# Expert weights in slots of 16 KB a partition, with the contraction order permuted to match

## The chip, the cores and the metric

The kernel runs on one core of one Trainium2 chip. The metric is the device time of one execution in microseconds (us). Profile times are counted from the first instruction. TensorE is called PE, VectorE DVE, ScalarE ACT, GpSimd POOL, and SyncE, which issues the large loads, SP. MiB are 1,048,576 bytes; the profile's MB are millions of bytes.

## The reference, cut to what matters

One residual block on 256 tokens of width 1024, all in float32: a mixer (gated linear attention beside banded attention, projections of 1024 x 8208 and 1024 x 1024), then 32 experts, then a small gated embedding and a norm.

```python
xn = rmsnorm(x, ln_mix); z = xn @ w_in            # mixer: w_in is 1024 x 8208
x = x + (sigmoid(gA) * y_a + sigmoid(gB) * y_b) @ w_out
xm = rmsnorm(x, ln_moe)                           # top 4 of 32 experts per token
for e in range(32):                               # w1[e]: 1024 x 2048, w2[e]: 1024 x 1024
    h = xm @ w1[e] + b1[e]
    out += gates[:, e:e+1] * (clamped_swiglu(h) @ w2[e] + b2[e])
x = x + out
x = x + sigmoid(rmsnorm(x, ln_ple) @ w_ple_gate) * (p @ w_ple_proj)
out = rmsnorm(x, ln_final)
```

An expert has 8 MiB of `w1` and 4 MiB of `w2`; the 32 have 384 MiB, all read once.

## The kernel before, in words

Each expert takes the up to 64 tokens that chose it. For expert e the order on PE, written out by hand, is: the bias (`h`, L750); the first layer (`h`, L758), 64 matmuls over eight slabs k of 128 rows of `w1`; transposes of small selectors (`t_st`); the scatter of expert e-1 (`acc`, L812); the gather of tokens for the next pair of experts (`t_g`, L725); the transposes of the activation (`t_a`, L776); and the second layer (`y`, L786), 32 matmuls over `w2`. Between `h` and `t_a` stands the gated unit on DVE and ACT (`glu`, L764 to L770).

Weights come through slots: SBUF tiles of 8 KB a partition (1 MiB), taken in a fixed cycle `order` from six pools (`N0` to `N5`: 1 + 5 + 3 + 4 + 6 + 2 = 21 slots). A slot of `w1` is one slab: partition p holds row 128k + p, one run of 8 KB in DRAM. A slot of `w2` holds two slabs: partition p holds rows p and p + 128 of a block of 256, two runs of 4 KB. SP issues all these loads in the program's order (L705 where a slot has two runs, L707 where it has one), and a load waits until the slot's last reader is done. The SBUF behind most slots belongs to the mixer's tiles first; `load_ahead` fills six slots while the mixer runs (L280), and the others come free as the mixer ends. The projections of the mixer stream through five of the same slots, in halves of a unit of 512 columns (`unit_steps`, L222; `out_weights`, L578). In the mixer's last part `out_prep(1)` transposes the second half of the gated sum (`t_h`, L567) and splits it into `hb`.

Expert 30 is preceded by the projection of `p` (`ple_proj`: `t_pT`, `t_pp`); the gate weights (4 MiB) follow expert 31, and `tail` does the rest. The branch for experts with more than 64 tokens (L1094) is not taken.

Of the kernel before, what the change touches and what calls it, by code (L numbers as in the profile page):

```python
# [64 lines left out]
def block_kernel(ctx: ExitStack, tc: tile.TileContext, x, p, ln_mix, w_in, w_gk, b_gk, gla_norm, rel_rev,  # L65
# [9 lines left out]
    ring0 = ctx.enter_context(tc.tile_pool(name="ring0", bufs=N0))  # L75
# [32 lines left out]
    # loads are issued in the order of the program  # L108
# [5 lines left out]
    # ------------------------------------------------------------------ mixer  # L114
    with ExitStack() as px:
# [12 lines left out]
        # the order of allocation puts what ends early under the slots that the experts take first  # L128
        # a place in the order of allocation for what comes to be allocated later
# [14 lines left out]
        lnr = wk.tile([16, P], F32, name="lnr")  # L144
# [29 lines left out]
        for i, a in enumerate((ln_moe, ln_ple)):  # L174
            nc.scalar.dma_start(lnr[8 * i:8 * i + 8, :], a.rearrange("o (k p) -> (o k) p", p=P))
# [7 lines left out]
        nc.gpsimd.dma_start(wr, w_router[0].rearrange("(k p) e -> p k e", p=P))  # L183
# [112 lines left out]
        with tc.tile_pool(name="gl", bufs=1, side="right") as gl:  # L296
# [15 lines left out]
            # low-rank forget gate  # L312
# [107 lines left out]
            load_ahead(N0, ring0)  # L420
# [118 lines left out]
        for i in range(4):  # L539
# [5 lines left out]
                                                         bhi[64:128, :].bitcast(F32), op=ALU.subtract))  # L545
        t0 = pa("t_ln2")
        nc.tensor.transpose(t0[:, 0:16], lnr, ident[0:16, 0:16])
        nc.vector.tensor_copy(lnT[:, 8:24], t0[:, 0:16])
# [63 lines left out]
        # residual, router  # L612
# [9 lines left out]
        def route_T(tb, half):  # L622
            t = pp("t_1")[:, 0, :].rearrange("p (k t) -> p k t", k=4)
            for j in range(4):
                k = 4 * half + j
                nc.tensor.transpose(t[:, j, :], x_sb[:, tb, k * P:k * P + P], ident)
            (nc.scalar.copy if half else nc.vector.tensor_copy)(x1T[tb][:, 4 * half:4 * half + 4, :], t)
# [58 lines left out]
    # ------------------------------------------------------------------ experts  # L686
# [8 lines left out]
    rest_of = [ring4, ring4, ring, ring4, ring, ring4, ring, ring4, ring4, ring, ring] + [ring3] * N3  # L695
    order = itertools.chain(rest_of, itertools.cycle([ring0] * N0 + [ring2] * N2 + [ring5] * N5 + rest_of))

    def slot_tile(dt, nm, pool=None):
        return (pool or next(order)).tile([P, 2048], dt, name=nm, tag="w")

    def slot(src, pool=None):
        w = slot_tile(F32, "w_raw", pool)
        n = src.shape[0] // P
        if n > 1:
            nc.sync.dma_start(w.rearrange("p (k c) -> p k c", k=n), src.rearrange("(k p) c -> p k c", p=P))  # L705
        else:
            nc.sync.dma_start(w, src)  # L707
        return w

    def expert_weights(e, k0=0):  # L710
        es_ = slice(e, e + 1) if isinstance(e, int) else bass.ds(e, 1)
        return ([slot(w1[0, es_, k * P:k * P + P, :].rearrange("o p c -> (o p) c")) for k in range(k0, KC)]
                + [slot(w2[0, es_, k * 256:k * 256 + 256, :].rearrange("o p c -> (o p) c")) for k in range(4)])
# [448 lines left out]
```

## Time and profile before

| | us |
|---|---|
| median of 3 runs | 1260.97 (1260.8 to 1262.39) |
| span of the profiled execution | 1259.5 |
| PE busy | 1151.8 (91%) |
| DVE busy | 374.1 (30%) |
| ACT busy | 262.8 (21%) |
| POOL busy | 37.2 (3%) |

The span is from the first instruction's start to the last one's end in the profiled execution; that execution's own time is not among the three runs, which stand 1.3 to 2.9 us above its span. A busy share is an average over stages with different limits: the mixer takes up to about 285 us, the experts up to 1220, the tail the rest.

### The profile page before, as it was taken

To read this page: it belongs to the slowest core of one execution; us is meant where nothing else is said; L and a number is where in the kernel's file an instruction comes from. 1 tells how busy PE (TensorE), PEld (TensorE's weight loads), DVE (VectorE), ACT (ScalarE), POOL (GpSimd) and SP (SyncE) were. 2 spreads that over 40 slices of the span, in tenths; PEclk is the share of its full clock that TensorE was granted. 3 is DMA by queue.
4 is the path that set the end of the run, shared out by engine and by line. 5 is a ranking of instruction groups with operands and counts; after the bars stand their busy time and mean duration, and the time that the engine had idled before them with its cause. 6 is when DMAs were issued, how large, how long until landed. Compare 5 with 4: busy or idle time off the path is not lost.

```text
span 1259.5 us, 15242 instructions
## 1 busy us (share of the span) xinstructions
PE 1151.8 (91%) x6314; PEld 575.8 (46%) x6314; DVE 374.1 (30%) x699; ACT 262.8 (21%) x464; POOL 37.2 (3%) x88
## 2 busy tenths in 40 slices
PE   6999999999999999999888888888888888888996
PEld 6988978874333433333333333333333333333345
DVE  5687476553111212112211111111111111111135
ACT  4756465541000100001000000000000000001025
POOL 2001010000000000000000000000000000000000
PEclk8999999989899999999999999999999999999898
DMA  9769778778999999999999999999999999999980
GB/s 279 223 124 287 218 152 224 283 286 340 395 419 416 416 416 417 417 416 417 417 417 417 417 417 418 417 417 417 417 417 417 418 417 417 417 416 417 417 325 35
DMA packets 95033, 454.32 MB, mean 361 GB/s; under 512 B 8488, under 2 KB 8656, under 8 KB 62192
## 3 DMA queue, kind: packets, MB, share of 16 engines
q1 hardware_dynamic: 91744, 447.51, 91.8%
q0 software_dynamic: 1840, 5.39, 1.7%
q8 instruction: 51, 0.84, 0.3%
q10 hardware_dynamic: 1376, 0.41, 0.2%
q14 instruction: 22, 0.18, 0.0%
HBM read 452.23 MB, written 1.05 MB: 360 GB/s over the span
## 4 chain that ended last, share of the span: by engine, by line
PE 58%; DMA 37%; ACT 2%; DVE 2%; issue 1%; SPq 0%; ACTq 0%
DMA w_raw<-in_w_dram 35%; PE h L758 16%; PE y L786 11%; PE t_g L725 4%; PE acc L812 2%; PE u_gB L247 2%; PE ax L592 2%; PE t_gate L1005 2%; PE u_ka L247 2%; DMA w_raw<-in_w_ple_gate_dram 2%; PE u_vg L251 1%; PE u_va L251 1%; PE u_qa L247 1%; PE u_gA L251 1%; PE u_qg L242 1%; ACT aT L778 1%
## 5 line engine op out<-in xcount | busy, mean ns | idle before, releaser
L758 PE MATMUL h<-w_raw,xT 128*64 128x512 f32 x2048 | 467.9, 599 | 54.8 <-DMA w_raw<-in_w_dram 54.8
L758 PEld LDWEIGHTS h<-w_raw,xT 128*64 128x64 f32 x2048 | 134.8, 136 | 370.5 <-issue 218.2
L786 PE MATMUL y<-w_raw,aT 128*64 128x512 f32 x1024 | 231.4, 605 | 23.0 <-ACT aT L778 23.0
L764 DVE TENSOR_SCALAR xg<-h 128x512 f32<-128x512 f32 x32 | 22.1, 692 | 495.6 <-PE h L758 495.6
L786 PEld LDWEIGHTS y<-w_raw,aT 128*64 128x64 f32 x1024 | 71.8, 139 | 162.4 <-issue 130.9
L803 ACT ACTIVATE jg<-t_st 128x256 f32<-128x256 f32 x32 | 12.3, 386 | 531.3 <-PE t_st L800 531.3
L791 DVE SCALAR_TENSOR_TENSOR yl<-y,gs,yh 128x512 fp32r<-128x512 f32 x32 | 24.0, 751 | 263.0 <-ACT yh L789 263.0
L126 DVE TENSOR_TENSOR wl<-w_raw,wh 128x1024 fp32r<-128x1024 f32 x68 | 83.2, 1224 | 49.9 <-ACT wh L126 49.5
L126 ACT CAST wh<-w_raw 128x1024 fp32r<-128x1024 f32 x68 | 71.2, 1047 | 68.0 <-PE u_ka L247 9.0
L789 ACT ACTIVATE yh<-y,gs 128x512 fp32r<-128x512 f32 x32 | 22.0, 688 | 234.6 <-PE y L786 234.6
L725 PE MATMUL t_g<-oh,x_sb 128*128 128x128 f32 x512 | 67.2, 287 | 0.0
L725 PEld LDWEIGHTS t_g<-oh,x_sb 128*128 128x128 f32 x512 | 61.6, 197 | 10.8 <-issue 10.2
L745 POOL CAST zs<-cb 128x128 fp32r<-128x128 f32 x32 | 9.5, 296 | 940.6 <-PE h L750 844.0
L778 ACT COPY aT<-t_a 128x512 f32<-128x512 f32 x32 | 18.8, 586 | 86.0 <-PE t_a L776 86.0
L812 PE MATMUL acc<-yh,st 64*128 64x512 f32 x124 | 28.2, 447 | 0.0
L812 PE MATMUL acc<-yl,st 64*128 64x512 f32 x124 | 25.2, 398 | 0.0
L729 DVE TENSOR_TENSOR xT<-t_g,lnT 128x512 f32<-128x512 f32 x32 | 22.1, 692 | 7.7 <-PE t_g L725 3.9
L750 PE MATMUL h<-BH,zs 128*128 128x512 f32 x64 | 24.2, 461 | 0.0
L797 DVE TENSOR_SCALAR go<-cb,posm,gates 128x128 f32<-128x128 f32 x64 | 21.6, 342 | 2.0 <-PE acc L870 2.0
L770 DVE TENSOR_TENSOR xlin<-xlin,sgm 128x512 f32<-128x512 f32 x32 | 21.9, 685 | 0.2
L769 DVE SCALAR_TENSOR_TENSOR xlin<-xlin,xg 128x512 f32<-128x512 f32 x32 | 21.8, 682 | 0.0
L768 DVE TENSOR_SCALAR xlin<-h 128x512 f32<-128x512 f32 x32 | 21.8, 681 | 0.0
(388 smaller groups left out, 1141.2 us busy)
## 6 DMA issues: line engine op xcount, KB each, us to landing
w_raw<-in_w_dram SPq DMA_DIRECT2D x384, 1024.0 KB, 19.9
w_raw<-in_w_in_dram SPq DMA_DIRECT2D x32, 1024.0 KB, 9.8
w_raw<-in_w_out_dram SPq DMA_DIRECT2D x4, 1024.0 KB, 4.9
w_raw<-in_w_ple_gate_dram SPq DMA_DIRECT2D x4, 1024.0 KB, 20.2
BT<-in_rel_bias_dram POOLq DMA_DIRECT2D x8, 256.0 KB, 6.6
x_sb<-in_x_dram SPq DMA_DIRECT2D x2, 512.0 KB, 5.0
BT<-in_rel_bias_dram POOLq DMA_DIRECT2D x8, 128.0 KB, 4.0
w_raw<-in_w_ple_proj_dram SPq DMA_DIRECT2D x1, 1024.0 KB, 20.8
```

Source lines behind the costliest of these rows:

```text
L126: return nc.scalar.copy(hi, full), nc.vector.tensor_tensor(lo, full, hi.bitcast(F32), op=ALU.subtract)
L247: nc.tensor.matmul(av[:, c, :], wt[:, kk % 2, c * P:c * P + P], xt[:, k, :], start=first and c % 2 == 0, stop=last, skip_group_check=True)
L251: nc.tensor.matmul(av[:, tb, :], xt[:, k, tb * P:tb * P + P], wt[:, kk % 2, :], start=first, stop=last)
L592: nc.tensor.matmul(ax[tb][dh], ht[:, tb, j, :], wt[:, dh * 512:dh * 512 + 512], start=hf == 0 and j == 0 and pi == 0, stop=hf == 1 and j = ...
L725: nc.tensor.matmul(t, x_sb[:, tb, k * P:k * P + P], oh[:, tb, :], start=first and tb == 0, stop=tb == 1, skip_group_check=True)
L750: nc.tensor.matmul(h[:, bk, :], zsel, BH[:, bk * 512:bk * 512 + 512], start=True, stop=False, skip_group_check=True)
L758: nc.tensor.matmul(h[64 * half:64 * half + 64, bk, :], stat(k), ws[k][:, c:c + 512], start=False, stop=k == KC - 1, skip_group_check=True)
L778: nc.scalar.copy(aT, t.rearrange("p (c s) -> p c s", c=4))
L786: nc.tensor.matmul(y[64 * dh:64 * dh + 64, :], aT[:, kk % 4, 64 * (kk // 4):64 * (kk // 4) + 64], w[:, kk % 2, dh * 512:dh * 512 + 512], s ...
L791: nc.vector.scalar_tensor_tensor(yl, y, gs, yh.bitcast(F32), op0=ALU.mult, op1=ALU.subtract)
L812: nc.tensor.matmul(dst[tb][dh], st[64 * dh:64 * dh + 64, tb * P:tb * P + P], y[64 * dh:64 * dh + 64, :], start=first and i == 0, stop=last ...
L1005: nc.tensor.matmul(t, xp[:, k, tb * P:tb * P + P], gp, start=k == 0 and i == 0, stop=k == KC - 1 and i == 2)
```

## The change

Slots become 16 KB a partition (2 MiB): ten of them (3 + 1 + 2 + 3 + 1), and 8 KB aside in `ring2` for `b2s` and `lfb`. One load fills a slot, and partition p takes neighbouring rows: 2p and 2p + 1 of a block of 256 rows of `w1`, 4p to 4p + 3 of a block of 512 rows of `w2`. In DRAM that is one run of 16 KB for each partition. An expert has six loads instead of twelve. The order of the contraction is permuted to match (`cols`): slab k now holds every second row, so the operands on the other side (`x_sb` in the gather and the router's transposes, `ln_moe` and `ln_ple`, the router's weights, `x2` and `y` in the transposed scatter) are read with a step of two, and the gated unit writes `a` with a step of four undone (`glu`). The projections of the mixer and `w_out` still come in 1 MiB loads, two to a slot. The matmuls are as many as before, and PE's order is the same up to the tail.

```diff
-N0, N1, N2, N3, N4, N5 = 1, 5, 3, 4, 6, 2
-AHEAD = (8, 12, 16)
+N1, N2, N3, N4, N5 = 3, 1, 2, 3, 1
+AHEAD = (8,)
+RJ = 2
+KM = KC // RJ
...
+    def cols(k, base=0):
+        m, j = divmod(k, RJ)
+        return slice(base + m * P * RJ + j, base + (m + 1) * P * RJ, RJ)
...
+            raws = ring.tile([P, KC, 512], F32, name="w_raw", tag="w")
             for half in range(2):
-                raw = ring.tile([P, 4, 512], F32, name="w_raw", tag="w")
+                raw = raws[:, 4 * half:4 * half + 4, :]
...
-                w = pool.tile([P, 2048], F32, name="w_raw", tag="w")
-                nc.sync.dma_start(w, w1[0, 0, k * P:k * P + P, :])
+                w = pool.tile([P, 4096], F32, name="w_raw", tag="w")
+                nc.sync.dma_start(w, w1[0, 0, k * 256:k * 256 + 256, :].rearrange("(p j) c -> p (j c)", j=RJ))
...
-            load_ahead(N0, ring0)
...
+        lnr = wk.tile([2 * KM, P * RJ], F32, name="lnr", tag="hf")
+        for i, a in enumerate((ln_moe, ln_ple)):
+            nc.gpsimd.dma_start(lnr[KM * i:KM * i + KM, :], a.rearrange("o (m q) -> (o m) q", m=KM))
...
-    rest_of = [ring4, ring4, ring, ring4, ring, ring4, ring, ring4, ring4, ring, ring] + [ring3] * N3
-    order = itertools.chain(rest_of, itertools.cycle([ring0] * N0 + [ring2] * N2 + [ring5] * N5 + rest_of))
+    rest_of = [ring4, ring, ring4, ring4, ring, ring] + [ring3] * N3
+    order = itertools.chain(rest_of, itertools.cycle([ring2] * N2 + [ring5] * N5 + rest_of))
...
+    def halves(dt, *nms):
+        w = slot_tile(dt, nms[0])
+        return w[:, 0:2048], w[:, 2048:4096]
+
+    def slot(src):
+        w = slot_tile(F32, "w_raw")
+        nc.sync.dma_start(w, src.rearrange("(p j) c -> p (j c)", p=P))
         return w
...
-            nc.tensor.matmul(t, x_sb[:, tb, k * P:k * P + P], oh[:, tb, :], start=first and tb == 0, stop=tb == 1,
+            nc.tensor.matmul(t, x_sb[:, tb, cols(k)], oh[:, tb, :], start=first and tb == 0, stop=tb == 1,
...
-                    c = half * 1024 + bk * 512
-                    nc.tensor.matmul(h[64 * half:64 * half + 64, bk, :], stat(k), ws[k][:, c:c + 512],
+                    c = k % RJ * 2048 + half * 1024 + bk * 512
+                    nc.tensor.matmul(h[64 * half:64 * half + 64, bk, :], stat(k), ws[k // RJ][:, c:c + 512],
...
-        nc.vector.tensor_tensor(xl_, xl_, sg, op=ALU.mult)
-        return xl_
+
+        a = mo.tile([P, 4, P], F32, name="a", tag="xg", bufs=1)
+        nc.vector.tensor_tensor(a, xl_.rearrange("s (p c) -> s c p", c=4), sg.rearrange("s (p c) -> s c p", c=4),
+                                op=ALU.mult)
+        return a
...
-        b2s = slot_tile(F32, "b2s")[0:NE, 0:D]
+        b2s = ring2.tile([P, 2048], F32, name="b2s", tag="s")[0:NE, 0:D]
...
-        return [slot(w_ple_gate[0, k2 * 256:k2 * 256 + 256, :]).rearrange("p (k c) -> p k c", k=2) for k2 in range(4)]
+        raw = []
+        for k4 in range(2):
+            raw.extend(halves(F32, "w_raw"))
+            for k2 in range(2 * k4, 2 * k4 + 2):
+                nc.sync.dma_start(raw[k2], w_ple_gate[0, k2 * 256:k2 * 256 + 256, :].rearrange("(p j) c -> p (j c)", p=P))
+        return [r.rearrange("p (k c) -> p k c", k=2) for r in raw]
```

Two places show how instructions move. The first is SP's queue where the mixer ends and the loads of the experts begin; `w_raw` numbers the slots' tiles, and the names in brackets are the counters a load waits for (`DVE`, `PE`: a reader of what lay in that memory; `DMAHW`: an earlier load). Before, from the last load of `w_out`:

```order
L578 DMA w_raw_2669<-in_w_out_dram 128x2x1024 [waits DMAHW0_49,DVE_49]
L707 DMA w_raw_2842<-in_w1_dram 128x2048 [waits DMAHW1_49,PE_49]
L707 DMA w_raw_2844<-in_w1_dram 128x2048 [waits DMAHW2_49]
L705 DMA w_raw_2846<-in_w2_dram 128x2x1024 [waits DMAHW4_49,DVE_49]
L705 DMA w_raw_2848<-in_w2_dram 128x2x1024 [waits DVE_49]
L705 DMA w_raw_2850<-in_w2_dram 128x2x1024 [waits DMAHW5_49,DVE_49]
L705 DMA w_raw_2852<-in_w2_dram 128x2x1024 [waits DMAHW6_49,PE_49]
L707 DMA w_raw_2991<-in_w1_dram 128x2048 [waits DMAHW7_49,DVE_49]
L707 DMA w_raw_2993<-in_w1_dram 128x2048 [waits DMAHW0_49,DVE_49,PE_49]
L707 DMA w_raw_2995<-in_w1_dram 128x2048 [waits DMAHW1_49,DVE_49]
```

The same place after the change:

```order
L592 DMA w_raw_2633<-in_w_out_dram 128x2x1024
L721 DMA w_raw_2815<-in_w1_dram 128x4096 [waits DVE_49,PE_49]
L721 DMA w_raw_2817<-in_w1_dram 128x4096 [waits DMAHW6_49,DMAHW5_49,DMAHW4_49]
L721 DMA w_raw_2819<-in_w2_dram 128x4096
L721 DMA w_raw_2821<-in_w2_dram 128x4096 [waits PE_49]
L721 DMA w_raw_2961<-in_w1_dram 128x4096 [waits DMAHW7_49,DMAHW0_49]
L721 DMA w_raw_2963<-in_w1_dram 128x4096 [waits DMAHW2_49,DMAHW1_49,DVE_49]
L721 DMA w_raw_2965<-in_w1_dram 128x4096 [waits PE_49]
L721 DMA w_raw_2967<-in_w1_dram 128x4096 [waits PE_49]
L721 DMA w_raw_2969<-in_w2_dram 128x4096 [waits DMAHW3_49,PE_49]
```

Before, the first of these loads waits for a matmul of the linear attention (`t_O`), and the load into `w_raw_2995` is the first to wait for the DVE instruction that finishes `hb`. After, the very first one (`w_raw_2815`) waits for that same DVE instruction, since its larger slot covers that memory too, and all later loads stand behind it.

The second place is ACT at expert 31 and the start of the tail: `yh` is the expert's output as ACT writes it, and `gh` the first split of the gate weights. Before:

```order
L766 ACTIVATE sgm<-xg 128x512
L778 COPY aT<-t_a 128x512
L789 ACTIVATE yh<-y,gs 128x512
L903 ACTIVATE gh<-w_raw,lnT 128x1024
L978 CAST x2h<-x2T 128x512 x2
```

After:

```order
L780 ACTIVATE sgm<-xg 128x512
L795 COPY aT<-t_a 128x512
L924 ACTIVATE gh<-w_raw,lnT 128x1024
L806 ACTIVATE yh<-y,gs 128x512
L999 CAST x2h<-x2T 128x512 x2
```

The split of the gate weights has moved ahead of `yh`, so ACT now reads the first gate weights before it takes the last expert's output.

## Rows read from the trace of the kernel before

**Rows 1.** The page: chain of work that ended last, by engine.
```profile
PE 58%; DMA 37%; ACT 2%; DVE 2%; issue 1%; SPq 0%; ACTq 0%
```

**Rows 2.** Busy time by stretch, last three columns: granted clock, DMA share, GB/s.
```profile
345.00:1145.00 800.00, 725.80 (x3532) 270.41 (x3529) 141.81 (x295) 62.39 (x138) 8.74 (x28) 1.00 1.02 417
```

**Rows 3.** PE's waits, 600 to 1260: us in total, times, longest.
```profile
PE h L758 <- DMA w_raw<-in_w_dram: 53.4, 91, 1.4
```

**Rows 4.** The chain in order of time: start, us, what.
```profile
388.54 7.09 PE y L786 x32
...
414.82 7.09 PE y L786 x32
...
930.13 1.12 PE acc L812 x8
...
960.25 1.13 PE acc L812 x8
```

**Rows 5.** DMA queue of SP, 345 to 1145: packets, MB, share of 16 engines.
```profile
q1 hardware_dynamic: 59404, 332.64, 101.4%
```

**Rows 6.** DMA of two stretches, 604 to 619 and 652.5 to 662.5: all packets, then SP's.
```profile
DMA packets 867, 6.31 MB, mean 421 GB/s; under 512 B 97, under 2 KB 97, under 8 KB 97
...
q1 hardware_dynamic: 867, 6.31, 101.2%
...
DMA packets 1014, 4.09 MB, mean 409 GB/s; under 512 B 63, under 2 KB 63, under 8 KB 968
...
q1 hardware_dynamic: 1013, 4.08, 101.8%
```

**Rows 7.** The page's queues: the one that loads instructions (packets, MB, share).
```profile
q8 instruction: 51, 0.84, 0.3%
```

**Rows 8.** The page's DMA issues: engine, count, KB each, us to landing.
```profile
w_raw<-in_w_dram SPq DMA_DIRECT2D x384, 1024.0 KB, 19.9
w_raw<-in_w_in_dram SPq DMA_DIRECT2D x32, 1024.0 KB, 9.8
w_raw<-in_w_out_dram SPq DMA_DIRECT2D x4, 1024.0 KB, 4.9
...
x_sb<-in_x_dram SPq DMA_DIRECT2D x2, 512.0 KB, 5.0
```

**Rows 9.** DMA queue of SP, 0 to 345.
```profile
q1 hardware_dynamic: 25850, 82.86, 77.1%
```

**Rows 10.** SP's issues by time: start, us, line, operation, count.
```profile
232.26 0.89 SPq L707 DMA_DIRECT2D w_raw<-in_w_dram  x2
...
254.85 0.33 SPq L707 DMA_DIRECT2D w_raw<-in_w_dram  x1
...
272.24 2.65 SPq L707 DMA_DIRECT2D w_raw<-in_w_dram  x3
...
287.00 0.38 SPq L705 DMA_DIRECT2D w_raw<-in_w_dram  x1
```

**Rows 11.** SP's waits, 190 to 300.
```profile
SPq L707 <- DVE hb L126: 1.8, 1, 1.8
```

**Rows 12.** Busy time by stretch, 285 to 288.
```profile
285.00:288.00 3.00, 3.00 (x15) 1.06 (x16) 2.86 (x15) 0.26 (x1) 0.00 (x0) 1.00 0.00 0
```

**Rows 13.** PE's instructions by time, 1113 to 1215; in brackets the idle time before.
```profile
1140.93 1.94 PE L758 MATMUL h<-w_raw,xT 128*64 128x512 f32 x8 [1.19 <-DMA w_raw<-in_w_dram]
...
1182.14 9.88 PE L786 MATMUL y<-w_raw,aT 128*64 128x512 f32 x32 [0.72 <-ACT aT L778]
...
1208.07 3.74 PE L832 MATMUL x2T<-cb,x 128*128 128x128 f32 x32
```

**Rows 14.** Groups by line, 345 to 1145: PE's weight loads, then DVE's.
```profile
L725 PEld LDWEIGHTS t_g<-oh,x_sb 128*128 128x128 f32 x439 | 51.1, 191 | 10.2 <-issue 10.2
...
L770 DVE TENSOR_TENSOR xlin<-xlin,sgm 128x512 f32<-128x512 f32 x27 | 18.5, 685 | 0.0
```

**Rows 15.** POOL's instructions by time, 0 to 345.
```profile
90.51 2.93 POOL L441 DMA_DIRECT2D BT<-in_rel_bias_dram  x4 [58.61 <-PE t_s L402]
```

More of the change, by code (lines that the diff above doesn't have):

```diff
@@ L143, in block_kernel @@
         wr = wk.tile([P, KC, NE], F32, name="wr")
-        lnr = wk.tile([16, P], F32, name="lnr")
+        wk.tile([P, P], F32, name="room0")
         kept("wh", 4)
@@ L545, in block_kernel @@
                                                          bhi[64:128, :].bitcast(F32), op=ALU.subtract))
+        lnr = wk.tile([2 * KM, P * RJ], F32, name="lnr", tag="hf")
+        for i, a in enumerate((ln_moe, ln_ple)):
+            nc.gpsimd.dma_start(lnr[KM * i:KM * i + KM, :], a.rearrange("o (m q) -> (o m) q", m=KM))
         t0 = pa("t_ln2")
-        nc.tensor.transpose(t0[:, 0:16], lnr, ident[0:16, 0:16])
-        nc.vector.tensor_copy(lnT[:, 8:24], t0[:, 0:16])
+        n2 = 2 * KM
+        for j in range(RJ):
+            nc.tensor.transpose(t0[:, j * n2:j * n2 + n2], lnr[:, j::RJ], ident[0:n2, 0:n2])
+        nc.vector.tensor_copy(lnT[:, 8:24].rearrange("p (i j) -> p j i", j=RJ),
+                              t0[:, 0:16].rearrange("p (j i) -> p j i", j=RJ))
         for k in range(KC):
@@ L624, in route_T @@
             for j in range(4):
-                k = 4 * half + j
-                nc.tensor.transpose(t[:, j, :], x_sb[:, tb, k * P:k * P + P], ident)
+                nc.tensor.transpose(t[:, j, :], x_sb[:, tb, cols(4 * half + j)], ident)
             (nc.scalar.copy if half else nc.vector.tensor_copy)(x1T[tb][:, 4 * half:4 * half + 4, :], t)
@@ L693, in pm @@
         return ps.tile([P, 512], F32, name=nm, tag="m", bufs=2)
-    rest_of = [ring4, ring4, ring, ring4, ring, ring4, ring, ring4, ring4, ring, ring] + [ring3] * N3
-    order = itertools.chain(rest_of, itertools.cycle([ring0] * N0 + [ring2] * N2 + [ring5] * N5 + rest_of))
+    rest_of = [ring4, ring, ring4, ring4, ring, ring] + [ring3] * N3
+    order = itertools.chain(rest_of, itertools.cycle([ring2] * N2 + [ring5] * N5 + rest_of))
     def slot_tile(dt, nm, pool=None):
[L699 to L707, printed above, removed]
+        return (pool or next(order)).tile([P, 4096], dt, name=nm, tag="w")
+    def halves(dt, *nms):
[4 more added lines that the diff above has]
+        nc.sync.dma_start(w, src.rearrange("(p j) c -> p (j c)", p=P))
         return w
@@ L711, in expert_weights @@
         es_ = slice(e, e + 1) if isinstance(e, int) else bass.ds(e, 1)
-        return ([slot(w1[0, es_, k * P:k * P + P, :].rearrange("o p c -> (o p) c")) for k in range(k0, KC)]
-                + [slot(w2[0, es_, k * 256:k * 256 + 256, :].rearrange("o p c -> (o p) c")) for k in range(4)])
+        return ([slot(w1[0, es_, k * 256:k * 256 + 256, :].rearrange("o p c -> (o p) c")) for k in range(k0, KM)]
+                + [slot(w2[0, es_, k * 512:k * 512 + 512, :].rearrange("o p c -> (o p) c")) for k in range(2)])
     def one_hots(e):
@@ L783, in second_layer @@
         for kk in range(8):
-            w = ws[8 + kk // 2].rearrange("p (k c) -> p k c", k=2)
+            w = ws[KM + kk // 4].rearrange("p (k c) -> p k c", k=4)
             for dh in range(2):
                 nc.tensor.matmul(y[64 * dh:64 * dh + 64, :], aT[:, kk % 4, 64 * (kk // 4):64 * (kk // 4) + 64],
-                                 w[:, kk % 2, dh * 512:dh * 512 + 512], start=kk == 0, stop=kk == 7)
+                                 w[:, kk % 4, dh * 512:dh * 512 + 512], start=kk == 0, stop=kk == 7)
         yh = mo.tile([P, 512], F32R, name="yh", tag="yh", bufs=1)
@@ L832, in rows_T @@
                 nc.tensor.matmul(dst[k // 2][:, (k % 2) * T + tb * P:(k % 2) * T + tb * P + P],
-                                 x2[:, tb, k * P:k * P + P], ident, start=k % 2 == 0 and tb == 0, stop=last,
+                                 x2[:, tb, cols(k)], ident, start=k % 2 == 0 and tb == 0, stop=last,
                                  skip_group_check=True)
@@ L873, in ple_proj @@
     def ple_proj():
-        pp_ = slot_tile(F32, "p_sb").rearrange("p (z b c) -> p z b c", z=4, b=2)
+        pp_, w = halves(F32, "p_sb")
+        pp_ = pp_.rearrange("p (z b c) -> p z b c", z=4, b=2)
         p_sb, pT = pp_[:, 0], pp_[:, 1]
         nc.gpsimd.dma_start(p_sb, p.rearrange("i b (t p) d -> p (i b t) d", p=P))
-        w = slot(w_ple_proj[0]).rearrange("p (k c) -> p k c", k=2)
-        ppj = slot_tile(F32, "ppj", ring2).rearrange("p (b c) -> p b c", b=2)
+        nc.sync.dma_start(w, w_ple_proj[0].rearrange("(p j) c -> p (j c)", p=P))
+        w = w.rearrange("p (k c) -> p k c", k=2)
         t = pm("t_pT")
@@ L898, in gate_split @@
         if j == 0:
-            wg.extend((slot_tile(F32R, "gh").rearrange("p (k c) -> p k c", k=2),
-                       slot_tile(F32R, "gl").rearrange("p (k c) -> p k c", k=2)))
+            wg.extend(t.rearrange("p (k c) -> p k c", k=2) for t in halves(F32R, "gh"))
         gh, gl_ = wg[-2:]
@@ L966, in tail @@
             wg.clear()
-            x2h = slot_tile(F32R, "x2h").rearrange("p (k t) -> p k t", k=KC)
-            x2l = slot_tile(F32R, "x2l").rearrange("p (k t) -> p k t", k=KC)
+            x2h, x2l = (t.rearrange("p (k t) -> p k t", k=KC) for t in halves(F32R, "x2h"))
             gate_split(raw, 0)()
@@ L981, in tail @@
                     gate_split(raw, (q + 1) // 2)()
-            x3 = slot_tile(F32, "x3").rearrange("p (b c) -> p b c", b=2)
-            x4 = slot_tile(F32, "x4").rearrange("p (b c) -> p b c", b=2)
+            x3, x4 = (t.rearrange("p (b c) -> p b c", b=2) for t in halves(F32, "x3"))
             sm = mo.tile([P, 164], F32, name="sm")
```

25 lines of the change are left out of this document (12 added, 13 removed).

## The prediction, made before the changed kernel ran

> **What bounds the kernel now.** I read the chain of waits first: PE has 58% of it and transfers 37% [rows 1], so both matter and the stages must be told apart. The view by stretches tells them apart: from 345 to 1145 us the DMA share is 1.02 at 417 GB/s, while PE is busy 725.8 of 800 us at a granted clock of 1.00 [rows 2]. The transfers never stop there. Until about 580 us PE eats from full slots: an expert takes it 414.82 - 388.54 = 26.28 us [rows 4]. Later it waits for weights, 53.4 us in 91 waits [rows 3], and an expert takes 960.25 - 930.13 = 30.12 us [rows 4]. SP's queue moved 332.64 MB in those 800 us [rows 5], which is 317.2 MiB, 2.522 us for a MiB or 30.26 us for an expert's 12 MiB. So the stream of weights sets when the last experts can start. PE has some 4 us of slack per expert; only behind the last starved matmuls, those at 1140.93 of expert 29 [rows 13], is PE's own work the path, and it needs all of the remaining time.
>
> **The time per MiB.** Loads of `w1` and `w2` pass one after the other, and two stretches show each nearly alone. From 604 to 619 (`w1`) SP's 867 packets took 101.2% of 16 engines x 15 us = 242.9 us; 97 are tiny, so 770 packets of 8 KB took 315 ns each, at 421 GB/s [rows 6]. From 652.5 to 662.5 (`w2`), 1013 packets took 162.9 us: 45 of 8 KB (14.2 us), 63 tiny ones, and 905 of 4 KB at 164 ns, at 409 GB/s [rows 6]. So 4 KB more cost 151 ns, and a packet costs some 13 ns besides. The change makes every expert packet 16 KB. No such packet from SP is in the trace, but the queue that loads instructions moved 0.84 MB in 51 packets, 16 KB each [rows 7], so the engines do take that size in one. Worked out, it takes 315 + 302 = 617 ns: per MiB an engine needs 4 x 617 = 2.47 us, against 8 x 315 = 2.52 (`w1`), 16 x 164 = 2.63 (`w2`) and 2.56 in the mix, a ratio of 0.966. By the rates instead: 421 GB/s is 2.491 us a MiB; 409, with the 9% of its bytes in 8 KB packets taken out, is 2.571; eight packets fewer per engine saved 0.080 us, so four fewer save 0.040: 2.451 against a mix of 2.518, ratio 0.973. Applied to 2.522: 2.435 and 2.455. I take the middle, **T = 2.445 us a MiB** (429 GB/s), 29.3 us an expert. From below the price is that of 8 KB packets throughout, 2.491/2.518 x 2.522 = 2.495; from above 2.435.
>
> The Trainium skill, HBM Reference, section Specifications (TRN2), gives a core that streams alone about 425 GB/s, bounded by its DMA engines, beside a per-core share of about 358. The trace is above that share, at 417. By 425 GB/s a MiB would take 2.467 us.
>
> **Where the stream starts.** This term goes the other way. By 345 us SP's queue had moved 82.86 MB [rows 9] = 79.0 MiB, of which 37 are the mixer's (32 + 4 loads of 1 MiB and `x`) [rows 8]: 42.0 MiB of experts. Before, the slots begin to fill at 232.26, and the load that waits for `hb` goes at 254.85 [rows 10, 11]. After the change the first load behind the mixer waits for that `hb`, and SP, being in order, holds the rest behind it: at 255 only 4 MiB lie ready (`load_ahead` fills two slots, before six of half the size). Six loads, 12 MiB, then go at once; the next two wait for the last matmuls of the mixer as before, at 272.24 [rows 10]; the next for the first slot that expert 0 frees, 287.00 before [rows 10] and one slab (1.9 us) later now. The 16 MiB keep the engines busy until 257 + 39 = 296, so the stream runs without a gap from 257, where before it stood still at 285 to 288 [rows 12] with all slots full. By 345 it has moved 4 + 88/2.445 = 40.0 MiB: 2 MiB, or 5 us, behind. No expert starves from that: expert 1's last `w1` slot lands by 298, and PE comes to expert 1 only past 285 + 26 = 311.
>
> **The sum.** Expert 29's last slab of `w1` is MiB 29 x 12 + 8 = 356. Before: 345 + 314.0 x 2.522 = 1136.9 (PE gets it at 1140.93; the landing and side loads are common to both). After: 257 + 352 x 2.445 = 1117.6, so -19.3 us. PE then has two slabs to multiply where it had one: +1.9 (8 matmuls, 1.94 us) [rows 13].
>
> Strided reads: in the stage they lie under PE's slack, 29.3 - 26.3 = 3 us an expert. Gather weight loads (191 ns) [rows 14], 16 an expert, could double and add 3.1 us, which that cover just holds; without it, 0.1 us x 27 experts = 3 us. Behind expert 29 nothing covers: the product into `a` (685 ns) [rows 14] for two experts, between 0 and +1.4 if it doubles, and the transposes of `x2` (3.74 us) [rows 13], between 0 and +3.7, most of which runs beside the gated unit. I take +0.7, nearest to no change, since contiguous rows are all the trace has and both ops are partly hidden.
>
> The Trainium skill, SBUF — State Buffer, section Door 1: The DMA port swizzle, gives lines of 16 bytes and a penalty for each access that crosses to a new one. The product into `a` reads with a step of 16 bytes, so by it the upper end of that bound is the likelier; no run here shows it yet.
>
> Costed at nothing: the `lnr` and `b2s` loads on POOL, which stood idle 58.61 us before the first `BT` [rows 15] (without that cover, about 0.7 us an issue, 2.93 for four); the permuted `w1` and `w2` operands, which stay contiguous runs of 512; the mixer, whose PE order is unchanged; `gh` ahead of `yh` on ACT, since the first gate MiB (386th) lands near 257 + 382 x 2.445 + 4 = 1195, before expert 31's `y` ends near 1203. If it were late, `yh`, the scatter and the tail would wait for it.
>
> -19.3 + 1.9 + 0.7 = -16.7. The profiled span of 1259.5 becomes 1242.8; the median of the runs shown stands 1.5 above that span, so **1244.3 us**.
>
> **Rivals.**
> - The engines work through 16 KB in pieces of 8 KB. For it: no SP packet above 8 KB was seen. T = 2.495: 257 + 352 x 2.495 = 1135.2, -1.7 + 1.9 + 0.7 = +0.9, about 1262: no change.
> - Slower: packets are not what costs; T stays 2.522 and only the late start is left. 257 + 352 x 2.522 = 1144.7, +7.8 + 2.6, about 1271. Against it: the two rates of rows 6. It decides from T above 2.490 on, so 16 KB packets must beat 8 KB ones.
> - Only part of the extrapolation comes true, a ceiling near 2.47: 1126.4, -10.5 + 2.6, about 1253. The Trainium skill's 425 GB/s (HBM Reference, as above) lies there.
> - PE's clock falls because each wait for a slot is longer (1.4 us every 4.9; before, 0.59 on average [rows 3]). At 1182.14 a `y` took 9.88 instead of 7.09 us after such an idle patch [rows 4, 13]. One such stretch an expert, +2.8, is still hidden (29.1 of 29.3); a second would make PE the bound and cost 2.6 x 27 = 69 us. Against it: waits up to 1.4 us left the clock at 1.00 [rows 2, 3].
>
> **How the numbers follow.** Forecast 0.60, ceiling 0.12, pieces 0.11, rate unchanged 0.11, clock 0.03, a longer mixer or another wait there 0.03. The forecast's own range is 1239 (T 2.435, no strided cost) to 1252 (2.455 and all strided costs). To leave out no more than 2 in 10, the range goes up to the pieces: 1237 to 1264. A measurement of this kernel tells some 0.2% (2.5 us) from no change: faster takes nearly all of forecast and ceiling and a little of the others, 0.74; same, mostly the pieces, 0.10; slower, the unchanged rate, the clock and a bad mixer, 0.16.
>
> **What would show it.** Right: SP's packets are 16 KB and take near 617 ns, the stage runs at 426 to 432 GB/s, an expert takes 29.3 us from well before 580 us on, the first load after `w_out` stands near 255 and the stream has no gap at 285, expert 29's last `h` starts near 1121, and PE waits about 1.4 us a slot at clock 1.00. Wrong: packets still of 8 KB, a rate of 417 or less, a mixer longer than 285 us, a granted clock below 1.00 in the stage, or `yh` of expert 31 waiting behind `gh`.

## The result, and the profile of the changed kernel

The changed kernel takes 1254.07 us (median of 5 runs, 1251.60 to 1255.23) against 1260.85 of the kernel before (5 runs): a ratio of 0.9938, interval 0.9922 to 0.9955. Forecast was 1244.3, with a range of its own from 1239 to 1252. Faster is right, but of the 16.7 us only 6.8 came between the medians. The profiled execution was the fastest of its five; its span is 1249.6, 9.9 below that of before and 6.8 above the 1242.8 forecast. The rows account for these 6.8 us. The other 3.0 between forecast and median are not in them: the median stands 2.5 above the profiled run, and each run's time 2.0 above its span, where the forecast had taken 1.5. A second group of five runs, beside the last experiments, gave 1251.57 (1250.63 to 1252.39; ratio 0.9927, interval 0.9914 to 0.9940).

First the chain of the page, by engine; it answers to [rows 1].

```profile
PE 49%; DMA 46%; DVE 2%; ACT 2%; issue 1%; SPq 0%; ACTq 0%
```

Then the stage from 345 to 1145 by stretch, columns as in [rows 2].

```profile
345.00:1145.00 800.00, 732.95 (x3590) 284.15 (x3588) 153.25 (x300) 65.36 (x140) 8.92 (x29) 1.00 1.01 427
```

SP's queue in the same stretch, and in the one from 0 to 345 (packets, MB, share), which answer to [rows 5, 9]; and SP's queue in a short stretch of the stage, 600 to 620, to be read as [rows 6].

```profile
q1 hardware_dynamic: 23487, 341.08, 100.3%
...
q1 hardware_dynamic: 21037, 79.15, 71.9%
...
DMA packets 583, 8.52 MB, mean 426 GB/s; under 512 B 63, under 2 KB 63, under 8 KB 63
q1 hardware_dynamic: 582, 8.50, 100.0%
```

The packets are of 16 KB: 519 of them in 320 engine-microseconds, 617 ns each (forecast 617). The stage runs at 427 GB/s at clock 1.00. 341.08 MB are 325.3 MiB, **2.459 us a MiB**; forecast was 2.445.

Next PE's wait for weights from 600 to 1250 (total, times, longest), and PE's instructions by time behind the last starved slots, as in [rows 3, 13].

```profile
PE h L772 <- DMA w_raw<-in_w_dram: 45.1, 38, 2.5
```

```profile
1129.90 3.65 PE L772 MATMUL h<-w_raw,xT 128*64 128x512 f32 x16 [1.24 <-DMA w_raw<-in_w_dram]
...
1172.04 0.66 PE L793 MATMUL t_a<-cb,a 128*128 128x128 f32 x4 [2.06 <-DVE a L786]
1173.37 8.79 PE L803 MATMUL y<-w_raw,aT 128*64 128x512 f32 x32 [0.68 <-ACT aT L795]
...
1198.18 3.93 PE L849 MATMUL x2T<-cb,x 128*128 128x128 f32 x32
```

Expert 29's last slot of `w1` is multiplied at 1129.90 (1140.93 before): 11.0 us earlier, where 19.3 were forecast. That is the miss. Behind it the program needs 1249.6 - 1129.9 = 119.7 us, before 1259.5 - 1140.9 = 118.6: +1.1, forecast +2.6.

The start of the stream: SP's issues by time, and two stretches ahead of and around the first of them (columns as in [rows 2]).

```profile
210.78 14.70 SPq L592 DMA_DIRECT2D w_raw<-in_w_out_dram  x4
257.28 72.05 SPq L721 DMA_DIRECT2D w_raw<-in_w_dram  x18
```

```profile
225.00:256.00 31.00, 30.95 (x143) 25.16 (x143) 18.95 (x24) 15.33 (x25) 0.00 (x0) 1.00 0.19 68
256.00:290.00 34.00, 32.04 (x170) 26.82 (x170) 17.96 (x50) 12.16 (x21) 0.58 (x2) 0.90 0.94 391
```

The first load behind the mixer goes at 257.28, 2.4 us later than `hb` let it go before [rows 10]; for 25 us ahead of it the stream stands still (68 GB/s; 307 before in the same stretch). By 345 SP's queue has moved 79.15 MB = 75.5 MiB, less the mixer's 37: 38.5 MiB of experts in place of the 40.0 forecast. That gives the landing of MiB 356: 345 + 317.5 x 2.459 = 1125.8, and PE comes 4.1 us behind it, as before. Against the forecast 1.5 MiB late are 3.7 us, and 316 x 0.0144 us another 4.6: the 8.3 that are missing.

### The profile page after: what moved, and what is told of

Read it like the earlier page. It is cut to its first block, busy times and chain, and to the rows that moved or that the text cites. A ratio compares the mean times of both kernels' runs of the same rounds, so it can differ in the third digit from the quotient of the medians.

```text
span 1249.6 us, 14906 instructions
## 1 busy us (share of the span) xinstructions
PE 1147.7 (92%) x6315; PEld 586.0 (47%) x6315; DVE 384.6 (31%) x699; ACT 264.5 (21%) x464; POOL 38.0 (3%) x90
## 4 chain that ended last, share of the span: by engine, by line
PE 49%; DMA 46%; DVE 2%; ACT 2%; issue 1%; SPq 0%; ACTq 0%
DMA w_raw<-in_w_dram 44%; PE h L772 15%; PE y L803 8%; PE t_g L739 2%; PE u_gB L255 2%; PE ax L606 2%; DMA w_raw<-in_w_in_dram 2%; PE u_ka L255 2%; PE u_qa L255 1%; PE u_vg L259 1%; PE u_va L259 1%; PE u_gA L259 1%; PE t_gate L1025 1%; PE acc L829 1%; PE u_rg L259 1%; PE u_kg L255 1%
## 5 line engine op out<-in xcount | busy, mean ns | idle before, releaser
L772 PE MATMUL h<-w_raw,xT 128*64 128x512 f32 x2048 | 455.4, 596 | 45.4 <-DMA w_raw<-in_w_dram 45.4
L772 PEld LDWEIGHTS h<-w_raw,xT 128*64 128x64 f32 x2048 | 140.4, 137 | 343.1 <-issue 253.5
L739 PE MATMUL t_g<-oh,x_sb 128*128 128x128 f32 x512 | 70.6, 294 | 0.0
L739 PEld LDWEIGHTS t_g<-oh,x_sb 128*128 128x128 f32 x512 | 65.0, 203 | 10.8 <-issue 10.2
L786 DVE TENSOR_TENSOR a<-xlin,sgm 128x512 f32<-128x512 f32 x32 | 34.9, 1090 | 0.2
L793 PE MATMUL t_a<-cb,a 128*128 128x128 f32 x128 | 20.6, 284 | 4.8 <-DVE a L786 2.1
L1025 PE MATMUL t_gate<-gh,x2h 128*128 128x512 f32 (+1 forms) x120 | 23.5, 352 | 0.5 <-DVE x2h L1000 0.5
```

The costliest lines, as they stand in the source:

```text
L739: nc.tensor.matmul(t, x_sb[:, tb, cols(k)], oh[:, tb, :], start=first and tb == 0, stop=tb == 1, skip_group_check=True)
L786: nc.vector.tensor_tensor(a, xl_.rearrange("s (p c) -> s c p", c=4), sg.rearrange("s (p c) -> s c p", c=4), op=ALU.mult)
L1025: nc.tensor.matmul(t, xp[:, k, tb * P:tb * P + P], gp, start=k == 0 and i == 0, stop=k == KC - 1 and i == 2)
```

## The experiments

Medians with lowest and highest; ratios are to the kernel before (1260.8 to 1261.0 in the three groups of runs).

| run | us | ratio, interval |
|---|---|---|
| small packets | 1275.27 (1273.63 to 1275.99) | 1.0115, 1.0100 to 1.0131 |
| before, `w2` neighbours | 1255.10 (1252.73 to 1255.74) | 0.9949, 0.9936 to 0.9963 |
| `ring` first | 1250.17 (1247.83 to 1252.35) | 0.9922, 0.9909 to 0.9936 |
| `lfb` last, `a` flat | 1251.78 (1249.27 to 1253.16) | 0.9927, 0.9914 to 0.9941 |
| 32 matmuls, 128 columns | 1255.68 (1254.13 to 1256.57) | 0.9956, 0.9941 to 0.9971 |
| 64 matmuls, 128 columns | 1274.08 (one run) | |
| all, 128 columns | 1253.78 (1252.03 to 1255.10) | 0.9942, 0.9929 to 0.9956 |
| changed kernel again | 1251.57 (1250.63 to 1252.39) | 0.9927, 0.9914 to 0.9940 |
| 32 matmuls, 32 columns | 1250.41 (1248.08 to 1253.27) | 0.9925, 0.9912 to 0.9938 |
| `ring` first, `lfb`, `a` | 1251.30 (1247.66 to 1252.67) | 0.9922, 0.9909 to 0.9935 |
| all, 32 columns | **1244.60** (1242.28 to 1247.66) | 0.9880, 0.9865 to 0.9895 |

The changed kernel's own two groups stand 2.5 us apart (1254.07, 1251.57), while those of the kernel before agree. Medians of two versions that are closer than that are not told apart by time; the rows must do it.

**The packet size alone.** In the changed kernel only the loads are undone (`load_ahead` likewise):

```diff
-        nc.sync.dma_start(w, src.rearrange("(p j) c -> p (j c)", p=P))
+        n = src.shape[0] // P
+        nc.sync.dma_start(w.rearrange("p (k c) -> p k c", k=n), src.rearrange("(k p) c -> p k c", p=P))
```

> The changed kernel with its slots of 16 KB, its pools and its order of loads, but every expert load reads its rows as before the change (each partition gets rows 128 apart), so that the packets are 8 KB for w1 and 4 KB for w2 again. The contraction order no longer fits the rows, so the output is another function of the weights; amount and timing of the work are untouched. Theory 1 (the packet size alone made the stage faster): 417 GB/s and 2.522 us a MiB return, MiB 356 comes 352 x (2.522 - 2.459) = 22 us later than in the changed kernel, time about 1276, that is 15 above the kernel before. Theory 2 (fewer and larger loads, or the order of the slots, made it faster): the stage stays near 427 GB/s and the time near 1254. A part each: between 1258 and 1272.

Measured: 1275.27. The stage by stretch, SP's queue in it, and expert 29's last slot:

```profile
345.00:1145.00 800.00, 721.87 (x3502) 275.82 (x3500) 148.82 (x292) 63.70 (x136) 9.00 (x29) 1.00 1.02 417
```

```profile
q1 hardware_dynamic: 56479, 332.86, 101.4%
```

```profile
1153.33 3.65 PE L774 MATMUL h<-w_raw,xT 128*64 128x512 f32 x16 [1.33 <-DMA w_raw<-in_w_dram]
```

417 GB/s are back. Slots twice the size and half as many loads give the stream nothing. So the change is two effects of opposite sign: 21.2 us gained by the packets (1275.27 to 1254.07), 14.3 lost by the rest (1260.98 to 1275.27), of which 12.4 stand by expert 29's last slot (1153.33 against 1140.93). By that slot the packets are worth 23.4 us (1129.90 in the changed kernel), where 22 were expected.

**Half of the packets, without the late start.** In the kernel before, `w2` alone is loaded with neighbouring rows (8 KB), and the transposes read every second column:

```diff
-            nc.tensor.transpose(t[:, c * P:c * P + P], a[:, c * P:c * P + P], ident)
+            m, j = divmod(c, 2)
+            nc.tensor.transpose(t[:, c * P:c * P + P], a[:, 256 * m + j:256 * m + 256:2], ident)
```

> The kernel before with one thing more: w2 is loaded with two neighbouring rows a partition (packets of 8 KB in its slots of 8 KB), and the four transposes of the activation read every second column. Slots, pools, order and start of the stream stay. If a packet costs a fixed 12 ns and 151 ns for each 4 KB, all at 8 KB gives 2.490 to 2.495 us a MiB in the stage in place of 2.522: 314 MiB x 0.027 to 0.032 = 8.5 to 10 us, time about 1251 (1249 to 1254), as fast as the whole change. If instead packets matter only from 16 KB on, or the mean of both kinds was already the limit: 1261. The transposes: 273 ns each if reading with a step costs PE nothing, more if it does (4 an expert, hidden in the stage).

Measured: 1255.10, 5.9 below before where 8.5 to 10 were expected, and outside the expected range. The stage, SP's queue in it, and PE's transposes in it:

```profile
345.00:1145.00 800.00, 732.61 (x3566) 277.88 (x3564) 144.33 (x300) 62.98 (x139) 8.98 (x29) 1.00 1.01 421
```

```profile
q1 hardware_dynamic: 46198, 335.71, 101.0%
```

```profile
L780 PE MATMUL t_a<-cb,xlin 128*128 128x128 f32 x112 | 18.7, 290 | 0.0
```

335.71 MB are 2.499 us a MiB, just outside the 2.490 to 2.495 expected; 0.023 x 314 = 7.2 us. A later start takes 1.4 of it: the first load behind the mixer went at 233.10 (before at 232.26 [rows 10]), and by 345 the queue had moved 82.29 MB (before 82.86 [rows 9]). The transposes took 290 ns where the kernel before has 273, so reading with a step costs PE a little. One edit with no new slots gives 5.9 us where the whole change gave 6.8 and 9.3 in its two groups.

**What a packet costs.** Nothing but the stream:

> Only the stream is left: no mixer, no experts, the output is x. Five phases of 48 MiB, one after the other, into five slots: w2 in packets of 4 KB, w1 in packets of 8 KB, w1 in 16 KB (loads of 2 MiB each), w1 in two runs of 16 KB a partition, w1 in one run of 32 KB (loads of 4 MiB). Theory 1 (a fixed 12.4 ns for a packet and 150.7 ns for each 4 KB, worked out from 163.4, 314.4 and 615.7 ns): 401 to 409 GB/s, 417 to 421, 426 to 428, the same, and 430 to 432 with 32 KB, the packets near 1218 ns. Theory 2 (427 is a ceiling for the core, whatever the packet): the last three phases are alike within 1 GB/s and the 32 KB packets are longer than 1218 ns, or cut into pieces. Theory 3 (PE's reads of the slots slow the stream): all phases are faster here than in the full kernels.

SP's queue in five inner stretches, 30 to 110 (4 KB), 150 to 230 (8 KB), 270 to 350 (16 KB), 370 to 460 (two runs of 16 KB) and 510 to 590 (32 KB):

```profile
DMA packets 8244, 32.77 MB, mean 410 GB/s; under 512 B 244, under 2 KB 244, under 8 KB 8244
q1 hardware_dynamic: 8244, 32.77, 102.6%
...
DMA packets 4374, 33.74 MB, mean 422 GB/s; under 512 B 256, under 2 KB 256, under 8 KB 256
q1 hardware_dynamic: 4374, 33.74, 101.2%
...
DMA packets 2364, 34.29 MB, mean 429 GB/s; under 512 B 271, under 2 KB 271, under 8 KB 271
q1 hardware_dynamic: 2364, 34.29, 100.7%
...
DMA packets 2497, 38.55 MB, mean 428 GB/s; under 512 B 144, under 2 KB 144, under 8 KB 144
...
DMA packets 1182, 34.54 MB, mean 432 GB/s; under 512 B 128, under 2 KB 128, under 8 KB 128
q1 hardware_dynamic: 1182, 34.54, 100.3%
```

Worked out as with [rows 6], the tiny packets counted in: 164, 315, 616 and 1218 ns. Each doubling adds 151, 301, 602: a straight line of some 14 ns a packet and 150.5 ns for each 4 KB. Theory 1 holds up to 32 KB; 427 is no ceiling, and beside PE's reads a packet takes as long (617 ns in the kernel). The shares fall as the packets grow: 102.6, 101.2, 100.7 and 100.3%, so consecutive small packets overlap more. The rate of the 16 KB phase, 34.29 MB in 80 us, is 2.446 us a MiB: the forecast's 2.445, which the kernel does not reach beside everything else. The slope is 16 x 4096 / 150.5 ns = 435 GB/s. The Trainium skill, DMA: Bandwidth & Descriptors, section Where 436 GB/s comes from, gives 435.2 GB/s for the ports of a core, and the slope agrees.

**The late start.** One line of the changed kernel:

```diff
-    rest_of = [ring4, ring, ring4, ring4, ring, ring] + [ring3] * N3
+    rest_of = [ring, ring, ring4, ring4, ring4, ring] + [ring3] * N3
```

> The changed kernel with one line other: expert 0 takes the two slots of `ring` that the mixer's weights leave first, and only then the three of `ring4`, of which the first waits for `hb`. Theory 1 (the late start costs what it was reckoned at, 2.46 us a MiB): the first two loads behind the mixer go near 240 and 251 in place of 257, 4 MiB early (-9.8 us); the 12 MiB behind them then run out near 289, 3 us before expert 0 frees a slot at 292, and 2 us of landing come on top (+5): net -4.8 us, about 1249 (1246 to 1252). Theory 2 (the start is hidden, since PE eats from full slots until 580 us): no change, 1254.

Measured: 1250.17. That is inside the range of theory 1, but so is the second group of the changed kernel, so the rows must decide. SP's issues by time, two stretches, and PE behind expert 29's last slot:

```profile
212.34 14.70 SPq L592 DMA_DIRECT2D w_raw<-in_w_out_dram  x4
241.06 57.84 SPq L721 DMA_DIRECT2D w_raw<-in_w_dram  x11
```

```profile
225.00:256.00 31.00, 30.95 (x141) 25.06 (x140) 18.70 (x22) 15.38 (x24) 0.00 (x0) 1.00 0.47 164
...
290.00:345.00 55.00, 52.91 (x236) 20.94 (x234) 11.72 (x27) 5.61 (x11) 0.86 (x2) 0.91 0.94 393
```

```profile
1127.89 3.65 PE L772 MATMUL h<-w_raw,xT 128*64 128x512 f32 x16 [1.23 <-DMA w_raw<-in_w_dram]
...
1171.37 7.09 PE L803 MATMUL y<-w_raw,aT 128*64 128x512 f32 x32 [0.68 <-ACT aT L795]
```

The first load goes 16 us earlier, and the gap behind 290 is there as reckoned (share 0.51 from 290 to 295). The last slot is 2.0 us earlier though this execution's mixer was 1.6 behind (212.34 against 210.78): 3.6 of the 4.8. The reckoning lacked a second pause, with a share of 0.74 from 340 to 345 and 0.90 from 345 to 350. There SP waits for expert 1's `y`, which took 9.05 us in place of 7.09, at a granted clock of 0.70 from 340 to 345. In the changed kernel the same `y` took 8.92 and the stream did not pause (0.99 and 1.02): only with the earlier start has the stream caught up with PE, which frees its slots. The rest of the lower span is another matter: expert 30's `y` took 7.09 here and 8.79 in the changed kernel.

**`lfb` and the product into `a`.** The load of `lfb` moves from POOL to SP behind `gate_raw()`, and

```diff
-        a = mo.tile([P, 4, P], F32, name="a", tag="xg", bufs=1)
-        nc.vector.tensor_tensor(a, xl_.rearrange("s (p c) -> s c p", c=4), sg.rearrange("s (p c) -> s c p", c=4),
-                                op=ALU.mult)
+        a = mo.tile([P, 512], F32, name="a", tag="xg", bufs=1)
+        nc.vector.tensor_tensor(a, xl_, sg, op=ALU.mult)
```

with transposes of `a[:, c::4]`.

> The changed kernel with two edits. The load of `lfb` (0.5 MiB), which the changed kernel issues on POOL at 334 us, goes on SP behind the last load of the program; before the change it came after 1145 us. And the product into `a` runs over contiguous rows again, while the four transposes read every fourth column. Theory 1: half a MiB less in the way of the experts' stream is 1.2 us; the product falls from 1093 to about 685 ns, which is 0.8 us for the two experts behind the stream, and the transposes stay within 20 ns of 279: 2 us in all, about 1252, and in the trace 0.5 MiB more of the experts' weights by 345 us than the start alone gives. Theory 2: both are hidden elsewhere, 1254. The time alone can hardly tell these; the rows must.

Measured: 1251.78, not to be told from the changed kernel. The product in the stage (DVE), first in the changed kernel, then here, with PE's transposes; then PE by time here.

```profile
L786 DVE TENSOR_TENSOR a<-xlin,sgm 128x512 f32<-128x512 f32 x28 | 30.6, 1093 | 0.0
```

```profile
L786 DVE TENSOR_TENSOR a<-xlin,sgm 128x512 f32<-128x512 f32 x28 | 19.1, 683 | 0.0
...
L792 PE MATMUL t_a<-cb,a 128*128 128x128 f32 x112 | 17.8, 281 | 0.0
```

```profile
1129.24 3.65 PE L772 MATMUL h<-w_raw,xT 128*64 128x512 f32 x16 [1.24 <-DMA w_raw<-in_w_dram]
...
1172.58 9.57 PE L802 MATMUL y<-w_raw,aT 128*64 128x512 f32 x32 [0.68 <-ACT aT L794]
```

Both terms are of the size expected. The step costs DVE 410 ns. It costs PE 2 ns a transpose (281 against 279), and the weight loads of these transposes, which run beside other work, take 204 ns against 140. By 345 SP's queue had moved 79.53 MB against 79.15, and the last slot is 0.7 us earlier, though the first load went 0.5 later (257.75). Both are lost again: `y` begins 0.8 earlier and ends at the same 1182.2, since it takes 9.57 in place of 8.79.

**PE's stop in the mixer.** The mixer was expected not to change, but in the changed kernel PE's timeline has a stop without a releaser, and the instruction queue a packet just ahead of its end (73 to 76):

```profile
76.16 0.39 PE L410 MATMUL t_s<-M 128*32 128x32 f32 x21 [1.72 <-issue]
```

```profile
q8 instruction: 1, 0.02, 2.0%
```

In the kernel before there is no such stop. To shift PE's program, 32 short matmuls on zeros were put ahead of it:

```diff
+            nc.vector.memset(room0, 0.0)
+            t_w = pa("t_w")
+            for i in range(32):
+                nc.tensor.matmul(t_w[:, 0:32], room0, room0[:, 0:32], start=True, stop=True)
```

> The changed kernel with 32 short matmuls on zeros ahead of PE's first transposes, where PE waits for its constants until 5.7 us; nothing reads them. All later instructions of PE stand 64 places further down its program. In the changed kernel PE stood still at 74.4 us for 1.7 us among the small matmuls `t_s` with no releaser in the profile, and a 16 KB packet of the instruction queue had begun at 73.9. Theory 1 (PE ran out of instructions there, at a place that depends on where the 16 KB blocks of its program begin): the stop goes elsewhere, shrinks or disappears, the mixer is up to 2 us shorter, time 1252 to 1254. Theory 2 (the stop belongs to this stretch, whatever stands where): it stays at `t_s` near 74 us with 1.7 to 2.7 us, 1254.

> As the run with 32 short matmuls, with 64 of them: PE's program stands 128 places further down. By theory 1 the stop without a releaser is at another place than without any and than with 32, or gone; by theory 2 it stands at `t_s` near 74 us in all three.

Measured: 1255.68 with 32, 1274.08 with 64. They ran far longer than meant (13.9 us for 32, 27.5 for 64), and the time with 64 is mostly that. With 32 the profile has no stop; with 64 it is back at the same matmuls:

```profile
PE t_s L414 <- issue: 3.3, 1, 3.3
```

The page counts 129 and 257 instructions more, not 64 and 128: each call is two matmuls and two weight loads. An estimate: if the instruction queue's 51 packets were all PE's, its 2 x 6315 instructions are 248 a packet, so 32 calls are half a packet and 64 a whole one. The run with 32 was made again with 32 columns of weights, which PE ends before its constants come, beside the changed kernel on the same chip:

> The changed kernel once more, beside the three others of this group on the same chip: 1254 (1252 to 1255). Whether PE's stop without a releaser at the small matmuls `t_s` and the half-clock stretch in expert 30's `y` (8.79 us) come again at the same places is read from its rows; if both belong to the program, they do, with 1.7 to 2.7 us and up to 2.8 us.

> The changed kernel with 32 short matmuls on zeros ahead of PE's first transposes as in the run before, but of 32 columns of weights in place of 128. There the 64 instructions of matmul and their weight loads took 13.9 us and put PE's first transposes 9 us later; these should be done before the constants come at 5.7 us. The shift of PE's program is the same. If the stop at `t_s` comes from where the blocks of PE's program begin: no stop there, and the first load behind the mixer goes some 2 us earlier than in the unshifted kernel, time 1252. If the stop was only pushed away by the late start: it is back with 1.7 to 2.7 us, 1254.

SP's issues of the changed kernel again, then with the shift; then PE of both by time.

```profile
257.60 2.52 SPq L721 DMA_DIRECT2D w_raw<-in_w_dram  x5
```

```profile
255.59 5.78 SPq L725 DMA_DIRECT2D w_raw<-in_w_dram  x6
```

```profile
1130.34 3.65 PE L772 MATMUL h<-w_raw,xT 128*64 128x512 f32 x16 [1.24 <-DMA w_raw<-in_w_dram]
...
1173.82 8.78 PE L803 MATMUL y<-w_raw,aT 128*64 128x512 f32 x32 [0.68 <-ACT aT L795]
```

```profile
1.07 3.62 PE L198 MATMUL t_w<-room 128*32 128x32 f32 x64 [1.07 <-DVE room L195]
...
1127.99 3.65 PE L776 MATMUL h<-w_raw,xT 128*64 128x512 f32 x16 [1.25 <-DMA w_raw<-in_w_dram]
...
1171.46 7.09 PE L807 MATMUL y<-w_raw,aT 128*64 128x512 f32 x32 [0.68 <-ACT aT L799]
```

The changed kernel stops again (2.2 us); with the shift nothing stops, the first load goes at 255.59 (254.85 before the change), and the last slot is 2.35 us earlier. That the stop depends on the place in PE's program is what half a packet (no stop there in four profiles) and a whole one (the stop is back, in one profile) show; that PE then waits for instructions is the likely reason, not a shown one. The medians, 1251.57 and 1250.41, overlap in their runs.

**All together.**

> The changed kernel with the slots of `ring` first, `lfb` last, the product into `a` contiguous, and the 32 short matmuls. If the gains add: 1250.2 - 1.2 - 0.8 = 1248.2, and down to 1246 if the stop of PE goes as well; against the kernel before a ratio of 0.988 to 0.990. If they hide each other: 1250.

> The changed kernel with the slots of `ring` first, `lfb` last and the product into `a` contiguous, without extra matmuls. If the gains of the two single runs add: 1250.2 - 1.2 - 0.8 = 1248.2. Where the half-clock stretch in expert 30's `y` takes back what comes in front of it, as between the changed kernel and the one with `lfb` last (1182.08 and 1182.09 at its end): 1250.

> All of it: `ring` first, `lfb` last, `a` contiguous, and the 32 short matmuls of 32 columns. If the stop of PE goes and the rest stays: 1.7 to 2.7 below the same kernel without the short matmuls, 1246; if the stop doesn't matter or comes back: the same as that one.

Measured: 1253.78 with the long matmuls (a miss: they delay the mixer, the first load goes at 244.40 in place of 241.06), 1251.30 without, 1244.60 with the short ones. The last stands 16.2 us below before: the fastest version here. SP's queue from 0 to 345, its first load, and PE by time:

```profile
q1 hardware_dynamic: 21263, 82.56, 74.9%
```

```profile
237.49 23.56 SPq L725 DMA_DIRECT2D w_raw<-in_w_dram  x6
```

```profile
1122.84 3.65 PE L776 MATMUL h<-w_raw,xT 128*64 128x512 f32 x16 [1.24 <-DMA w_raw<-in_w_dram]
...
1165.79 7.09 PE L806 MATMUL y<-w_raw,aT 128*64 128x512 f32 x32 [0.68 <-ACT aT L798]
```

82.56 MB by 345 are as many as before the change (82.86), now with 16 KB packets behind them. The version without short matmuls was expected at 1248 to 1250 and missed: its first load went at 244.15, 3.1 us behind that of `ring` first, with a granted clock of 0.91 from 25 to 45 us and 0.96 from 80 to 120, where `ring` first had 1.00. So of the 6.7 us between its first load and that of the best version, the stop is only some 2.3. The two differ again at the second pause. Expert 1's `y` and the stretch from 345 to 350 (last columns: granted clock, DMA share, GB/s), first without the short matmuls, then with them:

```profile
341.99 8.98 PE L802 MATMUL y<-w_raw,aT 128*64 128x512 f32 x32 [0.68 <-ACT aT L794]
...
345.00:350.00 5.00, 5.00 (x24) 1.56 (x22) 0.00 (x0) 0.00 (x0) 0.00 (x0) 0.92 0.41 115
```

```profile
335.14 7.09 PE L806 MATMUL y<-w_raw,aT 128*64 128x512 f32 x32 [0.68 <-ACT aT L798]
...
345.00:350.00 5.00, 5.00 (x26) 1.72 (x24) 0.00 (x0) 0.00 (x0) 0.00 (x0) 1.00 1.01 429
```

The load that waits for this `y` goes at 347.58 without them and at 338.83 with them, 8.7 us apart, and the last slot comes at 1130.54 and 1122.84, 7.7 apart. So a later mixer and a half-clock stretch in expert 1 make up most of the difference; whether the short matmuls have a hand in either clock stays open.

## Why the forecast was right in kind and too large

- **Packets of 16 KB at 617 ns**: right (617, and 616 alone), and the cause of the gain, as the small packets showed.
- **The time per MiB** is the larger mis-sized term: 2.459, not 2.445, which is 4.6 us. The durations were right; the step that failed is the ratio of durations, 0.966, "Applied to 2.522", which gave 2.435 and pulled the middle down. The 2.522 holds the overlap of the small packets, 101.4% by SP's share [rows 5]; those of 16 KB overlap only to 100.3%. The direct sum stood beside it: 4 x 617 ns = 2.47 us, and 2.47 / 1.003 = 2.46. The ratio of the rates, 0.973, was sound: its 2.455 is 0.004 short, 1.4 us. Alone the stream reaches 2.446, so the kernel loses half a per cent; the kernel before lost as much (2.522, where the phases of 4 and 8 KB alone make a mix of 2.511). Other queues' 0.77 MB in the stage are 0.2 per cent; where the rest goes stays open.
- **Where the stream starts** is the other: 38.5 MiB by 345, not 40.0, 3.7 us. The load that waits for `hb` went 2.4 us later, mostly because the mixer, which the forecast had put at nothing, stopped for 1.7 to 2.2 us (the shift took that away and left 0.7); this is the rival "a longer mixer", small. And `lfb`, half a MiB, was issued at 1153 before the change and at 334 after it, ahead of what PE waits for: 1.2 us. The forecast had priced POOL's issues of other loads, without naming `lfb`, and not whose bytes such loads delay.
- **The strided product** was put near nothing, with +1.4 as its upper bound: measured +0.8 (1093 ns for 685, twice). The Trainium skill, SBUF — State Buffer, section Door 1: The DMA port swizzle, with its lines of 16 bytes, had pointed to the upper end; 1.6 times is between the ends. The transposes of `x2` (3.93 against 3.74) and the gather's weight loads (197 ns in the stage against 191 [rows 14]) cost next to nothing, as taken.
- **Two slabs in the last slot**: 3.65 against 1.94 us, +1.7 (forecast +1.9).
- **What the sum did not have**: expert 30's `y`, in part at half clock, 9.88 us before [rows 13] and 8.79 after, gave 1.1 back. That is luck.
- **`gh` ahead of `yh`**: rightly put at nothing; `yh` of expert 31 let PE go on 0.79 us behind `y`, before and after.
- **Rivals.** Pieces of 8 KB and the unchanged rate are out. "A ceiling near 2.47", about 1253, comes nearest in number, but that is luck: as a mechanism it is out, since 32 KB packets ran at 432 GB/s. The 425 of the Trainium skill, HBM Reference, section Specifications (TRN2), is passed by 427 in this kernel. PE's clock stayed at 1.00 in the stage in spite of 1.2 us of waiting per slot. The lower end of the forecast's own range works out as 1240, not 1239.

## What to carry to other kernels

For a stream that bounds a kernel, add up packet durations (here 14 ns a packet and 150.5 ns for each 4 KB) and divide by the share that the queue shows for packets of that size (here 102.6% at 4 KB, falling to 100.3% at 32 KB); a ratio of durations laid on a measured rate carries the overlap of the old packets along. A coarser slot costs at the ends part of what longer packets gain in the middle (here 14.3 of 21.2 us): look for the first load that has to wait, and give it a slot that is free. Once the stream starts early enough to catch up with PE, a slow stretch of PE in the first experts delays it. Small loads on another queue that come free earlier go in front of the stream that is waited for, so put them behind it.

## What was not expected of the hardware

- PE stopped 1.7 to 3.3 us at one place of the mixer in seven profiles whose PE programs stand alike or a whole packet of instructions apart (the changed kernel twice, small packets, `ring` first, `lfb` last, `ring` first with both, and 64 matmuls), and not there with half a packet (in two of those four, 0.2 and 0.4 us at another place).
- Half-clock stretches come and go: expert 30's `y` took 7.09 us in four of the thirteen profiles and 8.78 to 9.99 us in the others, behind the same kind of idle patch (1.7 to 2.1 us for its input, then 0.7 for `aT`). In the changed kernel the granted clock from 1174 to 1176 was 0.50 (1.2 GHz), in `ring` first 1.00 throughout. A gain just ahead of such a stretch can be lost in it; what decides it was not found.
